# A two-block transformer kernel: the convolution in four segments, its order by hand, modulation loads placed anew, and a key normalisation queued behind the first scores

## The chip, the cores and the metric

The kernel runs on one core of one Trainium2 chip, all of it in fp32 accuracy. The metric is the device time of one execution in microseconds (us); before the change it is 986.46, the median of three runs (984.71 to 987.13). A measurement here is told apart from no change at about 0.3%.

## The reference

256 tokens of 1,024 channels go through a first block (stick-breaking attention, pooling and a gated unit, merged, then a feed-forward part) and through a second one of two layers. In layer 0 of the second block a conformer convolution mixes the tokens, in layer 1 an attention with 16 heads of 64 channels; each is followed by an MLP. Six modulation vectors per layer scale, shift and gate. Cut to what the change touches:

```
cond = silu(c)
mod = cond @ ada_w[i] + ada_b[i]                  # per layer: sh1, sc1, g1, sh2, sc2, g2
h = rms_norm(x, mix_norm_g[i]) * (1 + sc1) + sh1
# layer 0
a, g = split(h @ w_in + b_in, 2)
u = a * sigmoid(g)
u = causal depthwise convolution of u over the tokens, 31 taps, + dw_b
u = silu(layer_norm(u, ln_g, ln_b))
y = u @ w_out + b_out
# layer 1
q, k, v = split(h @ w_qkv, 3);  q, k = rms_norm per head
y = softmax(q k^T / 8 - slope * distance, causal) v @ w_o
x = x + g1 * y
h = rms_norm(x, mlp_norm_g[i]) * (1 + sc2) + sh2
x = x + g2 * (square(relu(h @ w1)) @ w2)
```

## The kernel before, in words

**Weights.** The 256 tokens are two tiles `t` of 128. All weights are streamed once, in halves of 1 MB: SP issues the load into one of three `raw` buffers (L335), ACT rounds it to `wH` (L364), DVE makes the rest `wL` (L365), and four pairs can be live. A product of accuracy fp32 is three fp32r matmuls per chunk of 128 rows: `wH` by the activations' high part (L464), `wL` by it (L465), `wH` by their low part (L466). `ts_job` (L531) is one such job, 128 tokens by 512 outputs over 1,024 inputs, 24 matmuls, with a bias row ahead of it in the convolution (`bias_rows`, L541).

**Modulation.** `ada_w` makes 48 more halves of the same stream. Each is multiplied by `cond` and summed on DVE, two accumulations of 128x1024 (L393). Where a group is complete, `ada_finish` brings it to a row by four matmuls with 32 output columns (L405) and sends it through DRAM; `ada_load` brings it back on 128 partitions. The table `PUSH` says how many such halves are queued behind which weight blocks.

**Convolution.** `hk` holds h. For two halves `n` of the channels and two token tiles there are a gate and a linear job (`cg`, `ca`); `glu` (L1071) multiplies them into `uu[n]`. The 31 taps are applied in a Fourier basis: `conv_fwd` transforms a segment of 128 tokens by plain fp32 matmuls (L1080), DVE multiplies the spectrum by the taps' cosine and sine tables (L1086, two products), and `conv_inv` transforms back (L1095), accumulating two matmuls per tile and segment onto the bias row. Three overlapping segments cover the tokens, so that a tile meets two of them: four pairs of tile and segment, eight forward and sixteen inverse matmuls, all 128x128 by 512 columns. `normed` (L1111) normalises a tile, `to_chan` transposes it (L1117), applies silu (L1121) and splits it for the output projection `co` (`two_by_two`, L903). In this stretch PE's order is written out by hand (`manual_schedule`); DVE's and ACT's are a scheduler's, by priority. `conv_load` (L919) brings the tables in during the feed-forward part of the first block and makes the taps' spectra by four matmuls of 31 rows (L931).

**Attention.** `qk_norm` (L1211) squares on ACT, sums on DVE, takes the power on POOL (L1217) and multiplies on DVE (L1219); `qk_trans` transposes. `at_scores` (L1234) makes a pair of heads' scores on PE (L1242), adds the distance on DVE (L1246), takes maxima (L1248, L1249), exponentials on ACT (L1250, L1251) and scales (L1253, L1254); `at_trans` transposes the result (L1263); `av` multiplies by v with 64 output columns a head (L1313, L1314).

## Time and profile before

| | us |
|---|---|
| median of three runs (lowest, highest) | 986.46 (984.71, 987.13) |
| profiled execution, its own time | 986.63 |
| its span | 984.9 |
| PE busy | 961.7, 98% of the span |
| DVE busy | 709.1, 72% |
| ACT busy | 545.3, 55% |

The rows further below come from the profiled execution. In a timeline a row is: start in us, duration in us, engine, line, operation, output<-inputs, tile (rows*columns and moving operand for PE), type, number of records run together, and in brackets the idle time before it and what ended it. A plain fp32 matmul makes two records, an fp32r one makes one. Matmuls overlap in the pipeline, so that the distance between two starts tells what one costs, not its duration. The granted clock (PEclk) is a share of TensorE's full 2.4 GHz; 0.5 is 1.2 GHz.

### The profile page before, as it was taken

What the parts mean: (1) busy time and instruction counts of PE and PEld (TensorE: products, weight loads), DVE (VectorE), ACT (ScalarE), POOL (GpSimd) and SP (SyncE); (2) the same over time, 40 slices, a digit from 0 to 9 for tenths busy, and PEclk for the clock granted to TensorE, in tenths of its full rate; (3) what the DMA queues carried; (4) which work ended last, traced back from release to release, by engine and by line L of the source; (5) the groups of instructions that cost most, each with busy time, mean ns of one, the idle gap of its engine ahead of it and who ended that gap; (6) DMA issues with size and microseconds to landing.
All of it is one profiled execution on the core that took longest, in us unless ns stands there. A gap on an engine that the chain in (4) does not pass through costs nothing.

```text
span 984.9 us, 12815 instructions
## 1 busy us (share of the span) xinstructions
PE 961.7 (98%) x4969; PEld 790.5 (80%) x4969; DVE 709.1 (72%) x914; ACT 545.3 (55%) x835; POOL 61.0 (6%) x88
## 2 busy tenths in 40 slices
PE   7999999999999999998999999999999999999998
PEld 5998889878788887874878888887876778888886
DVE  6768878787587777887677677768578576665553
ACT  5656764556555565523545655555576456555561
POOL 5002110010000000100000000001320000000000
PEclk9999999999899999999999999999999999999999
DMA  7887786579478986685258888875525356676531
GB/s 251 275 287 260 260 282 227 171 257 331 147 273 304 312 300 203 235 308 195 86 171 302 286 282 290 297 267 185 195 83 164 108 171 214 224 251 253 192 128 43
DMA packets 89732, 223.37 MB, mean 227 GB/s; under 512 B 4305, under 2 KB 8299, under 8 KB 89671
## 3 DMA queue, kind: packets, MB, share of 16 engines
q1 hardware_dynamic: 89670, 222.55, 65.6%
q8 instruction: 39, 0.64, 0.3%
q14 instruction: 23, 0.18, 0.1%
HBM read 221.44 MB, written 1.10 MB: 226 GB/s over the span
## 4 chain that ended last, share of the span: by engine, by line
PE 82%; DVE 10%; issue 2%; POOL 2%; ACT 2%; DMA 1%; POOLq 0%; SPq 0%; ACTq 0%
PE A L466 14%; PE A L464 14%; PE A L465 14%; PE B L479 14%; PE B L480 7%; PE A L479 5%; DVE wL L365 4%; PE A L480 2%; PE A L471 2%; PE A L472 2%; PE A L473 2%; POOL rst L549 1%; PE A L1095 1%; PE B L524 1%; DVE rs L568 1%
## 5 line engine op out<-in xcount | busy, mean ns | idle before, releaser
L365 DVE TENSOR_TENSOR wL<-raw,wH 128x1024 fp32r<-128x1024 f32 x306 | 362.0, 1219 | 122.0 <-ACT wH L364 120.8
L364 ACT ACTIVATE wH<-raw 128x1024 fp32r<-128x1024 f32 x306 | 307.3, 1051 | 186.9 <-PE A L466 119.3
L479 PE MATMUL B<-hHL,wH 128*128 128x512 f32 x576 | 204.1, 398 | 0.0
L480 PE MATMUL B<-hHL,wL 128*128 128x256 f32 x576 | 161.8, 281 | 0.0
L464 PE MATMUL A<-wH,hidH 128*128 128x512 f32 x384 | 152.3, 397 | 0.0
L466 PE MATMUL A<-wH,hidL 128*128 128x512 f32 x384 | 150.8, 393 | 0.0
L465 PE MATMUL A<-wL,hidH 128*128 128x512 f32 x384 | 150.6, 392 | 0.0
L464 PE MATMUL A<-wH,hHL 128*128 128x512 f32 (+1 forms) x336 | 130.9, 390 | 1.5 <-ACT wH L364 0.8
L479 PEld LDWEIGHTS B<-hHL,wH 128*128 128x128 f32 x576 | 108.3, 188 | 27.5 <-ACT wH L364 0.8
L465 PE MATMUL A<-wL,hHL 128*128 128x512 f32 (+1 forms) x336 | 129.0, 384 | 0.5 <-DVE wL L365 0.5
L466 PE MATMUL A<-wH,hHL 128*128 128x512 f32 (+1 forms) x336 | 129.5, 386 | 0.0
L393 DVE SCALAR_TENSOR_TENSOR acc<-raw,cond,acc 128x1024 f32<-128x1024 f32 x84 | 107.7, 1282 | 10.7 <-DMA raw<-in_ada_w_dram 9.8
L480 PEld LDWEIGHTS B<-hHL,wL 128*128 128x128 f32 x576 | 108.8, 189 | 0.7
L464 PEld LDWEIGHTS A<-wH,hidH 128*128 128x128 f32 x384 | 72.8, 190 | 18.9 <-issue 3.8
L466 PEld LDWEIGHTS A<-wH,hidL 128*128 128x128 f32 x384 | 72.6, 189 | 15.9
L465 PEld LDWEIGHTS A<-wL,hidH 128*128 128x128 f32 x384 | 72.9, 190 | 14.6
L464 PEld LDWEIGHTS A<-wH,hHL 128*128 128x128 f32 x336 | 63.6, 189 | 14.9 <-ACT wH L364 1.2
L465 PEld LDWEIGHTS A<-wL,hHL 128*128 128x128 f32 x336 | 63.8, 190 | 12.8 <-DVE wL L365 1.0
L466 PEld LDWEIGHTS A<-wH,hHL 128*128 128x128 f32 x336 | 63.8, 190 | 12.5 <-DVE hHL L519 0.4
L479 PE MATMUL A<-hHL,wH 128*128 128x512 f32 x192 | 68.1, 399 | 0.0
L986 ACT ACTIVATE rs<-B 128x256 f32<-128x256 f32 x72 | 27.1, 377 | 49.9 <-PE B L480 49.8
L480 PE MATMUL A<-hHL,wL 128*128 128x256 f32 x192 | 53.6, 279 | 0.0
(238 smaller groups left out, 1167.0 us busy)
## 6 DMA issues: line engine op xcount, KB each, us to landing
raw<-in_mlp_w_dram SPq DMA_DIRECT2D x64, 1024.0 KB
raw<-in_ada_w_dram SPq DMA_DIRECT2D x48, 1024.0 KB
raw<-in_w_in_dram SPq DMA_DIRECT2D x19, 1024.0 KB
raw<-in_w_ff_in_dram SPq DMA_DIRECT2D x16, 1024.0 KB
raw<-in_w_ff_out_dram SPq DMA_DIRECT2D x16, 1024.0 KB
raw<-in_attn_w_qkv_dram SPq DMA_DIRECT2D x12, 1024.0 KB
raw<-in_conv_w_in_dram SPq DMA_DIRECT2D x8, 1024.0 KB
ada<-mod SPq DMA_DIRECT2D x24, 256.0 KB
```

Of the source, the lines that this page charges most:

```text
L364: act(h[:, p:q, :], v[:, p:q, :], AF.Copy)
L365: nc.vector.tensor_sub(l[:, p:q, :], v[:, p:q, :], h[:, p:q, :].bitcast(F32))
L393: stt(acc, v[:, c, :], cond[:, k:k + 1], src, op0=ALU.mult, op1=ALU.add)
L464: mm(dst, lh(xc), wh, start=s0, stop=False)
L465: mm(dst, lh(xc), wl, start=False, stop=False)
L466: mm(dst, ll(xc), wh, start=False, stop=s1)
L471: mm(dst, wh, rh(xc), start=(i == 0), stop=False)
L472: mm(dst, wh, rl(xc), start=False, stop=False)
L473: mm(dst, wl, rh(xc), start=False, stop=(i == len(kcs) - 1))
L479: mm(dst, wh, km.HL[:, :, k, :], start=(k == 0), stop=False)
L480: mm(dst[:, 0:S], wl, km.HL[:, 0, k, :], start=False, stop=(k == KC - 1))
L986: act(r1[:, s, :], a[:, S:2 * S], AF.Copy)
```

## The change

The convolution takes four segments that each keep 64 tokens and do not share them: a segment's window is its 64 tokens and the ones before it. Segment 2 needs tokens of both tiles, so DVE copies the wanted halves of the products into a tile `mid` on the way. Each segment is one forward matmul per channel half; the inverse of a tile is four matmuls of 64 output columns, two segments by cosine and sine, onto the two halves of the rows. DVE and ACT follow the hand-written order too, two jobs are cut by an argument `mid=(cut, fn)`, and `pump(1)`, `limit=` place the weight steps. Modulation halves are queued elsewhere: two instead of six in the convolution, one more in the MLP's list, three behind the blocks of v; the load of layer 1's third segment moves behind the attention. The tables of the convolution lie and are loaded otherwise. In the attention one exponential of a single element stands ahead of the stage, and the last multiply of a normalisation is queued behind the first pair's maxima (`issue_after`). The diff, cut to its core; a line "..." stands for what is left out (the tables' contents, and removed code that the listing above shows):

```diff
@@ -30,20 +30,18 @@
-PUSH = {'pre': (0, 1, 0, 0, 0, 0), 'mix': (1, 2, 1, 2, 2, 1), 'ff': (1, 1, 1, 1, 1, 1, 1, 1, 1, 0, 1, 1, 1, 1, 1, 1), 'conv': (1, 4, 1), 'mlp': (1, 1, 1, 0, 1, 1, 1, 1, 1, 1, 1, 0, 1, 1, 0, 1), 'at': (0, 0, 0, 0)}
+PUSH = {'pre': (0, 1, 0, 0, 0, 0), 'mix': (1, 2, 1, 2, 2, 1), 'ff': (1, 1, 1, 1, 1, 1, 1, 1, 1, 0, 1, 1, 1, 1, 1, 1), 'conv': (0, 2, 0), 'mlp': (1, 1, 1, 0, 1, 1, 1, 1, 1, 1, 1, 1, 1, 1, 0, 1), 'at': (0, 0, 0, 0)}
-KEEP = SEG - PAD
+KEEP = 64
+NSEG = S // KEEP
...
@@ -249,6 +245,7 @@
             ada_push(PUSH["at"][2 * n + i])
     for n in range(2):
         B["av", n] = block512(I["attn_w_qkv_2"], 3 * D, 2 * D + n * 512)
+    ada_push(3)
     for n in range(2):
         B["ao", n] = block512(I["attn_w_o_2"], D, n * 512)
     for j in range(9):
@@ -528,11 +525,16 @@
                 self.from_token_half(t, b, src[b])
-    def ts_job(km, t, blk, n0=0, n1=512, bias=None):
+    def ts_job(km, t, blk, n0=0, n1=512, bias=None, mid=None):
         dst = bankA()
         if bias is not None:
             bias_rows(dst, bias)
-        ts(dst[:, :n1 - n0], km.h(t), km.l(t), blk, K8, n0, n1, start=bias is None)
+        cut = mid[0] if mid else KC
+        ts(dst[:, :n1 - n0], km.h(t), km.l(t), blk, K8[:cut], n0, n1, start=bias is None, stop=not mid)
+        if mid:
+            mid[1]()
+            ts(dst[:, :n1 - n0], km.h(t), km.l(t), blk, K8[cut:], n0, n1, start=False)
         return dst
...
@@ -900,12 +903,13 @@
-    def two_by_two(km, b0, b1, after, bias=(None, None)):
-        res = {}
+    def two_by_two(km, b0, b1, after, bias=(None, None), res=None):
+        res = dict(res or {})
         need(b0, b1)
         for t in range(NT):
             for n, b in enumerate((b0, b1)):
-                res[t, n] = ts_job(km, t, b, bias=bias[n])
+                if (t, n) not in res:
+                    res[t, n] = ts_job(km, t, b, bias=bias[n])
                 if t == 1:
                     if n == 0:
                         after(0, [res[0, 0], res[0, 1]])
@@ -918,19 +922,21 @@
     def conv_load():
         tb = I["conv_tables"]
-        cv["tab"] = T([P, TS_], "q4", 4)
-        nc.sync.dma_start(cv["tab"], dram(tb, 0, [[TI, P], [1, TS_]]))
-        cv["inv"] = T([P, len(PAIRS), 2, P], "gb", 2)
-        nc.sync.dma_start(cv["inv"], dram(tb, TS_, [[TI, P], [2 * P, len(PAIRS)], [P, 2], [1, P]]))
         dw = T([P, D], "q4", 4)
         nc.sync.dma_start(dw[:TAPS, :], dram(I["conv_dw_2"], 0, [[D, TAPS], [1, D]]))
-        cv["w"] = [T([P, D], "q4", 4) for _ in range(2)]
-        for j in range(2):
-            for n in range(2):
+        aux = T([P, TI - TF], "rs", 4)
+        nc.sync.dma_start(aux, dram(tb, TF, [[TI, P], [1, TI - TF]]))
+        cv["w"] = [T([P, 2, 512], "q4", 4)]
+        tab = T([P, TF], "q4", 4)
+        nc.sync.dma_start(tab, dram(tb, 0, [[TI, P], [1, TF]]))
+        cv["fwd"] = tab[:, :NSEG * P].rearrange("p (b n) -> p b n", b=NSEG)
+        cv["inv"] = tab[:, NSEG * P:].rearrange("p (t j n) -> p t j n", t=NT, j=2)
+        cv["w"].append(T([P, 2, 512], "q4", 4))
+        for n in range(2):
+            for j in range(2):
                 pt = bankB()
-                mm(pt, cv["tab"][:TAPS, TF + j * P:TF + (j + 1) * P], dw[:TAPS, n * 512:(n + 1) * 512],
-                   start=True, stop=True)
-                act(cv["w"][j][:, n * 512:(n + 1) * 512], pt, AF.Copy)
+                mm(pt, aux[:TAPS, j * P:(j + 1) * P], dw[:TAPS, n * 512:(n + 1) * 512], start=True, stop=True)
+                act(cv["w"][n][:, j, :], pt, AF.Copy)
         raw = T([P, 512], "rs", 4)
         for h in range(2):
             r = h * NB
@@ -1062,114 +1068,122 @@
     uu = [T([P, NT, 512], "hidH", 2) for _ in range(2)]
+    mid = T([P, 2, 512], "ok", 2)
     outs = {}
     spec = {}
...
+    SPEC_AT = {(0, 0): ("hidL", 2), (0, 1): ("hidL", 2), (0, 2): ("ok", 2), (0, 3): ("gb", 2),
+               (1, 0): ("q4", 4), (1, 1): ("q4", 4), (1, 2): ("ok", 2), (1, 3): ("ok", 2)}
+    def gate_of(t, n, **kw):
+        sg = ts_job(hk, t, B["cg", n], bias=2 + n, **kw)
+        g = T([P, 512], "rs", 4)
+        act(g, sg, AF.Sigmoid)
+        return g
+    def glu(t, n, g):
+        a = ts_job(hk, t, B["ca", n], bias=n)
+        vtt(uu[n][:, t, :], a, g, op=ALU.mult)
+        r = slice(KEEP - KEEP * t, P - KEEP * t)
+        vtt(mid[r, n, :], a[r, :], g[r, :], op=ALU.mult)
+    def conv_fwd(n, b):
+        s = bankB()
+        mm(s, cv["fwd"][:, b, :], mid[:, n, :] if b == 2 else uu[n][:, b // 2, :], start=True, stop=True)
+        pr = spec[n, b] = T([P, 2, 512], *SPEC_AT[n, b])
         for j in range(2):
...
+            vtt(pr[:, j, :], s, cv["w"][n][:, j, :], op=ALU.mult)
     st6 = [T([P, 2, 6], "bn", 2) for _ in range(NT)]
     tn = {}
+    def conv_inv(t, n):
+        o = outs[t, n] = bankB() if t else bankA()
+        bias_rows(o, 4 + n)
+        for j in range(2):
+            for i in range(2):
+                cs = slice(i * KEEP, (i + 1) * KEEP)
+                mm(o[cs, :], cv["inv"][:, t, j, cs], spec[n, 2 * t + i][:, j, :], start=False, stop=(j == 1))
     def stats(t, n):
         nc.vector.bn_stats(st6[t][:, n, :], outs[t, n])
...
+    def rstd(t):
         mv = T([P, 2], "ss", 4)
         nc.vector.bn_aggr(mv, st6[t])
...
+        tn[t] = mv, rstd_of([mv[:, 1:2]])
+    def normed(t):
+        mv, rs = tn[t]
+        tn[t] = []
         for b in range(2):
...
+            h = T([P, 512], "rs", 4)
+            vts(h, outs[t, b], mv[:, 0:1], rs, op0=ALU.subtract, op1=ALU.mult)
+            tn[t].append(h)
+    def to_chan(t, b):
+        pt = bankB()
+        for i in range(4):
+            nc.tensor.transpose(pt[:, i * P:(i + 1) * P], tn[t][b][:, i * P:(i + 1) * P], ident)
+        sl = T([P, 4, P], "rs", 4)
+        for i in range(4):
+            c = 4 * b + i
+            act(sl[:, i, :], pt[:, i * P:(i + 1) * P], AF.Silu, scale=col("lng", c), bias=col("lnb", c))
+        sk.split(sl, 4 * b, 4 * b + 4, t * P, (t + 1) * P)
+    ada_load(0, 4)
+    sk = KM((("hidL", "hidL"), ("hidH", "gb")))
+    co = {}
+    need(B["cg", 0], B["ca", 0])
+    with tc.manual_schedule(engines={nc.tensor.engine, nc.vector.engine, nc.scalar.engine}):
         for t in range(NT):
...
+            g = gate_of(t, 0)
             if t == 1:
...
+                done(B["cg", 0], limit=2)
+            glu(t, 0, g)
+        done(B["ca", 0], limit=2)
+        g = gate_of(0, 1)
+        for b in range(NSEG):
+            conv_fwd(0, b)
+        glu(0, 1, g)
+        for t in range(NT):
+            conv_inv(t, 0)
+            stats(t, 0)
+        pump(1)
         conv_fwd(1, 0)
...
+        conv_fwd(1, 1)
+        pump(1)
+        def inv01():
+            conv_inv(0, 1)
+            stats(0, 1)
+            rstd(0)
+        g = gate_of(1, 1, mid=(6, inv01))
+        done(B["cg", 1], limit=1)
+        normed(0)
+        glu(1, 1, g)
+        done(B["ca", 1], limit=1)
+        to_chan(0, 0)
         conv_fwd(1, 2)
...
+        conv_fwd(1, 3)
+        to_chan(0, 1)
+        pump(1)
+        def inv11():
+            conv_inv(1, 1)
+            stats(1, 1)
+            rstd(1)
+        co[0, 0] = ts_job(sk, 0, B["co", 0], bias=6, mid=(4, inv11))
+        pump(1)
         normed(1)
...
+        def chan1():
+            to_chan(1, 0)
+            to_chan(1, 1)
+        co[0, 1] = ts_job(sk, 0, B["co", 1], bias=7, mid=(6, chan1))
+    pump()
@@ -1180,7 +1194,7 @@
     ada_load(0, 3)
-    two_by_two(sk, B["co", 0], B["co", 1], after_mix(0), bias=(6, 7))
+    two_by_two(sk, B["co", 0], B["co", 1], after_mix(0), bias=(6, 7), res=co)
@@ -1190,7 +1204,6 @@
     ff(nk[-1], (("m1", 0), ("m2", 0)), after_mlp0,
        {2: lambda: ada_load(0, 5), 6: lambda: ada_load(1, 1, 0)})
-    ada_load(1, 2)
@@ -1204,6 +1217,7 @@
+    act(ada_one[0:1, 0:1], ada_one[0:1, 0:1], AF.Exp, scale=0.0)
@@ -1215,10 +1229,14 @@
         nc.vector.reduce_sum(ssq, sq.rearrange("p (h d) -> p h d", d=64), axis=AX.X)
         nc.gpsimd.tensor_scalar(ssq, ssq, EPS, None, op0=ALU.add)
         nc.gpsimd.tensor_tensor(ssq, ssq, neg_half.to_broadcast([P, 8]), op=ALU.pow)
-        qq = T([P, 512], "rs", 4)
-        vtt(qq.rearrange("p (h d) -> p h d", d=64), a.rearrange("p (h d) -> p h d", d=64),
-            ssq.rearrange("p (h o) -> p h o", o=1).to_broadcast([P, 8, 64]), op=ALU.mult)
-        return qq
+        def scaled():
+            qq = T([P, 512], "rs", 4)
+            vtt(qq.rearrange("p (h d) -> p h d", d=64), a.rearrange("p (h d) -> p h d", d=64),
+                ssq.rearrange("p (h o) -> p h o", o=1).to_broadcast([P, 8, 64]), op=ALU.mult)
+            return qq
+        return scaled
@@ -1246,7 +1264,9 @@
             stt(s, dist, -slopes[h], z[:, :384], op0=ALU.mult, op1=ALU.add)
             m = T([P, 2], "ss", 4)
             nc.vector.reduce_max(m[:, 0:1], s[:, 0:P], axis=AX.X, negate=True)
-            nc.vector.reduce_max(m[:, 1:2], s[:, P:384], axis=AX.X, negate=True)
+            top = nc.vector.reduce_max(m[:, 1:2], s[:, P:384], axis=AX.X, negate=True)
+            if i == 1 and state["top"] is None:
+                state["top"] = top
             act(s[:, 0:P], s[:, 0:P], AF.Exp, bias=m[:, 0:1], accum_out=sums[:, 0, h:h + 1])
             act(s[:, P:384], s[:, P:384], AF.Exp, bias=m[:, 1:2], accum_out=sums[:, 1, h:h + 1])
             nc.vector.reciprocal(sums[:, :, h:h + 1], sums[:, :, h:h + 1])
@@ -1267,7 +1287,7 @@
-    state = {"s": 0, "t": 0, "o": 0}
+    state = {"s": 0, "t": 0, "o": 0, "top": None}
@@ -1294,10 +1314,15 @@
                 if t == 1:
                     done(b)
                 flush(HOLD)
-                pend.append((n, t, i, qn))
+                state["top"] = None
                 if n == 1 and t + i > 0:
                     for _ in range(2):
                         at_step(8)
+                if state["top"] is None:
+                    pend.append((n, t, i, qn()))
+                else:
+                    with tc.issue_after(state["top"].ins):
+                        pend.append((n, t, i, qn()))
@@ -1338,7 +1363,7 @@
     while state["o"] < 16:
         at_step(16)
         av_next(16)
-    ada_load(1, 4, 3)
+    ada_load(1, 2, 4, 3)
     two_by_two(ok, B["ao", 0], B["ao", 1], after_mix(1))
```

Where rows move, three places. First PE in the convolution, the first inverse matmuls and what stands around them (`uu` is hidH, the spectra are rs before, and hidL, ok and gb now; the bias row is brow). Before:

```order
L466 MATMUL A_3878<-wH_3736,hHL_3490 128x512
L1080 MATMUL B_3920<-hidH_3638,q_367_2446 128x512
L1095 MATMUL A_3874<-rs_3870,gb_2448 128x512
L1095 MATMUL A_3874<-rs_3872,gb_2448 128x512
L541 MATMUL A_3929<-brow_2481,pick_2473 128x512
L1095 MATMUL A_3929<-rs_3870,gb_2448 128x512
L1095 MATMUL A_3929<-rs_3872,gb_2448 128x512
L1080 MATMUL B_3933<-hidH_3639,q_367_2446 128x512
L541 MATMUL A_3939<-brow_2481,pick_2473 128x512
```

Now:

```order
L463 MATMUL A_3837<-wH_3781,hHL_3490 128x512
L543 MATMUL A_3865<-brow_2481,pick_2473 128x512
L1105 MATMUL A_3865<-hidL_3819,q_370_2451 64x512
L1105 MATMUL A_3865<-hidL_3824,q_370_2451 64x512
...
L543 MATMUL B_3872<-brow_2481,pick_2473 128x512
L1105 MATMUL B_3872<-ok_3829,q_370_2451 64x512
L1105 MATMUL B_3872<-gb_3834,q_370_2451 64x512
...
L1091 MATMUL B_3883<-hidH_3635,q_370_2451 128x512
L1091 MATMUL B_3888<-hidH_3635,q_370_2451 128x512
L543 MATMUL A_3897<-brow_2481,pick_2473 128x512
```

Before, a tile's inverse stands in pieces between jobs, each matmul 128 columns wide; now its four 64-column ones follow each other on one bias row, both tiles in a row, ahead of the forward matmuls of the other channel half.

Second DVE in the convolution, from the spectra of column half 1 to the normalisation of the first tile (wL is a weight step, acc a modulation accumulation, bn the statistics, A and B are PSUM banks). Before:

```order
L1086 TENSOR_TENSOR rs_3978<-B_3975,q_370_2452 128x512
L1086 TENSOR_TENSOR rs_3980<-B_3975,q_371_2453 128x512
L1086 TENSOR_TENSOR rs_3984<-B_3982,q_370_2452 128x512
L1086 TENSOR_TENSOR rs_3986<-B_3982,q_371_2453 128x512
L1103 BN_STATS bn_3643<-A_3971 128x6
L1107 BN_AGGR ss_3991<-bn_3643 128x2
L548 TENSOR_SCALAR rst_3993<-ss_3991 128x1
L1111 TENSOR_SCALAR hidL_3996<-A_3874,ss_3991,rst_3993 128x512
L1111 TENSOR_SCALAR hidL_3996<-A_3971,ss_3991,rst_3993 128x512
L1103 BN_STATS bn_3644<-A_3999 128x6
```

Now, the statistics and spectra, and further on the product for `mid` (ok) with its spectra:

```order
L1108 BN_STATS bn_3638<-A_3865 128x6
L1108 BN_STATS bn_3639<-B_3872 128x6
L390 SCALAR_TENSOR_TENSOR acc_3402<-raw_3743,cond_84,acc_3402 128x1024 x2
L1094 TENSOR_TENSOR q_599_3885<-B_3883,q_371_2453 128x512 x2
L1094 TENSOR_TENSOR q_601_3890<-B_3888,q_371_2453 128x512 x2
L390 SCALAR_TENSOR_TENSOR acc_3402<-raw_3779,cond_84,acc_3402 128x1024 x2
L1108 BN_STATS bn_3638<-A_3917 128x6
...
L1085 TENSOR_TENSOR hidH_3635<-A_3949,rs_3935 128x512
L1087 TENSOR_TENSOR ok_3637<-A_3949,rs_3935 64x512
L362 TENSOR_TENSOR wL_3978<-raw_3881,wH_3977 128x1024 x2
L516 TENSOR_TENSOR hidL_3996<-rs_3990,hidL_3995 128x4x128
L1094 TENSOR_TENSOR ok_4001<-B_3999,q_371_2453 128x512 x2
```

The accumulations now stand in front of the spectra of column half 1 and of the last statistics of tile 0, and two weight steps and a split stand between `mid` and its spectra.

Third DVE in the attention, at the first pair of heads (w are the scores, ss the maxima, ssq the norms). Before:

```order
L1215 TENSOR_REDUCE ssq_6058<-junk_6059 128x8
L1219 TENSOR_TENSOR rs_6064<-A_6033,ssq_6058 128x512
L1246 SCALAR_TENSOR_TENSOR w_965_6078<-cst_5806,B_6072 128x384
L1246 SCALAR_TENSOR_TENSOR w_967_6088<-cst_5806,B_6073 128x384
L1248 TENSOR_REDUCE ss_6080<-w_965_6078 128x1
L1249 TENSOR_REDUCE ss_6080<-w_965_6078 128x1
...
L1246 SCALAR_TENSOR_TENSOR w_971_6104<-cst_5806,B_6098 128x384
L1246 SCALAR_TENSOR_TENSOR w_973_6114<-cst_5806,B_6099 128x384
```

Now:

```order
L1229 TENSOR_REDUCE ssq_6046<-junk_6047 128x8
L1264 SCALAR_TENSOR_TENSOR w_959_6064<-cst_5793,B_6058 128x384
L1264 SCALAR_TENSOR_TENSOR w_961_6074<-cst_5793,B_6059 128x384
L1266 TENSOR_REDUCE ss_6066<-w_959_6064 128x1
L1267 TENSOR_REDUCE ss_6066<-w_959_6064 128x1
L1266 TENSOR_REDUCE ss_6076<-w_961_6074 128x1
L1267 TENSOR_REDUCE ss_6076<-w_961_6074 128x1
L1264 SCALAR_TENSOR_TENSOR w_965_6090<-cst_5793,B_6084 128x384
...
L1267 TENSOR_REDUCE ss_6102<-w_967_6100 128x1
L1235 TENSOR_TENSOR rs_6116<-A_6021,ssq_6046 128x512
```

The multiply (rs<-A,ssq) that stood ahead of the first pair's scores now stands behind the second pair's maxima.

## Rows read from the trace of the kernel before

**Rows 1.** The page, engines: busy time, share of the span, instructions.
```profile
PE 961.7 (98%) x4969; PEld 790.5 (80%) x4969; DVE 709.1 (72%) x914; ACT 545.3 (55%) x835; POOL 61.0 (6%) x88
```

**Rows 2.** PE's waits: who waits for whom; total us, times, longest.
```profile
PE B L524 <- DVE rs L575: 4.0, 5, 1.2
```

**Rows 3.** PE's timeline through the convolution.
```profile
393.33 0.40 PE L541 MATMUL A<-brow,pick 128*128 128x512 f32 x1
...
399.02 0.40 PE L541 MATMUL A<-brow,pick 128*128 128x512 f32 x1
...
450.44 1.88 PE L1095 MATMUL A<-rs,gb 128*128 128x512 f32 x4
452.24 0.50 PE L541 MATMUL A<-brow,pick 128*128 128x512 f32 x1
...
457.88 1.98 PE L1095 MATMUL A<-rs,gb 128*128 128x512 f32 x4 [0.85 <-DVE rs L1086]
...
466.43 0.50 PE L464 MATMUL A<-wH,q 128*128 128x512 f32 x1 [1.56 <-ACT q L518]
468.43 0.66 PE L1117 MATMUL B<-ident,hidL 128*128 128x128 f32 x4 [1.50 <-DVE hidL L1111]
...
492.36 0.39 PE L464 MATMUL A<-wH,hHL 128*128 128x512 f32 x1
```

**Rows 4.** PE's timeline at four matmuls of 32 output columns.
```profile
277.80 1.06 PE L405 MATMUL B<-acc,onesr 128*32 128x512 f32 x8
278.80 0.50 PE L464 MATMUL A<-wH,hidH 128*128 128x512 f32 x1
279.13 0.39 PE L465 MATMUL A<-wL,hidH 128*128 128x512 f32 x1
```

**Rows 5.** PE's timeline in the product with v, 64 output columns.
```profile
773.39 0.65 PE L1313 MATMUL A<-q,gb 128*64 128x256 f32 x4
773.82 0.44 PE L1314 MATMUL A<-q,gb 128*64 128x128 f32 x4
```

**Rows 6.** ACT's timeline at the convolution's first silu.
```profile
457.90 1.28 ACT L1121 ACT_TABLE_LOAD   x1 [4.77 <-DVE rs L1086]
464.00 1.85 ACT L1121 ACTIVATE rs<-B,cols 128x128 f32<-128x128 f32 x5 [4.82 <-PE B L1117]
```

**Rows 7.** Line L393: durations min/median/max in ns; its waits in us, times.
```profile
L393 DVE SCALAR_TENSOR_TENSOR acc<-raw,cond,acc x84: 1265/1277/1422, 52.7 to 896.1; 128x1024 f32<-128x1024 f32 x84
...
  DMA raw<-in_ada_w_dram: 11.0, 7
```

**Rows 8.** Timelines of DVE, ACT and PE at the attention's first pair.
```profile
716.96 0.69 DVE L1219 TENSOR_TENSOR rs<-A,ssq 128x512 f32<-128x512 f32 x1 [2.11 <-POOL ssq L1217]
717.57 1.01 DVE L1246 SCALAR_TENSOR_TENSOR w<-cst,B 128x384 f32<-128x384 f32 x2
...
718.85 1.28 ACT L1250 ACT_TABLE_LOAD   x1 [4.14 <-DVE ss L1248]
...
716.23 0.50 PE L465 MATMUL A<-wL,hHL 128*128 128x512 f32 x1
...
719.80 0.39 PE L465 MATMUL A<-wL,hHL 128*128 128x512 f32 x1
721.99 0.61 PE L1263 MATMUL B<-ident,w 128*128 128x128 f32 x3 [1.80 <-DVE w L1253]
```

**Rows 9.** Stretches: length, busy us (instructions) of PE, PEld, DVE, ACT, POOL; PEclk, DMA share, GB/s.
```profile
252.00:258.00 6.00, 6.00 (x13) 4.13 (x13) 4.29 (x5) 2.93 (x5) 0.00 (x0) 0.50 0.80 281
722.00:726.00 4.00, 4.00 (x14) 3.17 (x15) 3.08 (x11) 3.52 (x12) 0.00 (x0) 0.58 0.00 0
768.00:776.00 8.00, 8.00 (x62) 6.30 (x61) 5.22 (x5) 6.63 (x10) 0.00 (x0) 1.00 0.36 110
```

**Rows 10.** PE's timeline at the taps' four matmuls.
```profile
248.57 4.26 PE L931 MATMUL B<-q,q 31*128 31x512 f32 x8
```

More of the change, by code (lines that the diff above doesn't have):

```diff
@@ L710, in net_kernel @@
         rs = rstd_of([ssg[:, t:t + 1]])
-        stt(gvt[:, t, :], gvt[:, t, :], rs, gmg, op0=ALU.mult, op1=ALU.mult)
-    done(B["gv"])
+        last = stt(gvt[:, t, :], gvt[:, t, :], rs, gmg, op0=ALU.mult, op1=ALU.mult)
+    with tc.issue_after(last.ins):
+        done(B["gv"])
     need(B["u"])
@@ L1089, in conv_inv @@
-    def conv_inv(t, n, b):
-        i = PAIRS.index((t, b))
-        if (t, n) not in outs:
-            outs[t, n] = bankA()
-            bias_rows(outs[t, n], 4 + n)
-        for j in range(2):
-            mm(outs[t, n], cv["inv"][:, i, j, :], spec[n, b, j], start=False, stop=(j == 1 and b == t + 1))
-    ada_load(0, 4)
-    sk = KM((("q4", "q4"), ("q4", "q4")))
+    SPEC_AT = {(0, 0): ("hidL", 2), (0, 1): ("hidL", 2), (0, 2): ("ok", 2), (0, 3): ("gb", 2),
+               (1, 0): ("q4", 4), (1, 1): ("q4", 4), (1, 2): ("ok", 2), (1, 3): ("ok", 2)}
```

117 lines of the change are left out of this document (19 added, 98 removed).

## The prediction

> **What bounds it now.** I read the page first: PE is busy 961.7 us of the span of 984.9, DVE 709.1 [rows 1]. So the end is set by the amount of PE work plus the places where PE stands, and DVE and ACT matter only where PE waits for them. The view of PE's waits came next: the named waits are few and short, the costliest group 4.0 us over five [rows 2], in places that the change leaves alone. Those it touches are single: three in the convolution [rows 3] and one in the attention [rows 8], each under 2 us. Then PE's timeline through the convolution, from the first bias row (393.33) to the first matmul of the following MLP (492.36): 99.0 us [rows 3].
>
> What this stretch holds, by rows: twelve jobs of a bias row and 24 matmuls, 5.69 us each from bias row to bias row (393.33 to 399.02), 68.3 in all. Four inverse matmuls from 450.44 to the bias row at 452.24 take 1.80, less 0.08 of settling: 0.43 for each of two passes, 0.86 for a plain fp32 matmul with 512 moving columns. Sixteen of these are 13.8 us, the eight forward ones 6.9. Of the rest, 0.85 + 1.56 + 1.50 = 3.9 us are idle before the rows at 457.88, 466.43 and 468.43 [rows 3].
>
> **The change, part by part, against the profiled execution of 986.63 us** (0.17 above the median of the three runs, 986.46).
>
> *Narrow inverse matmuls.* Still sixteen of 512 moving columns, but each now fills 64 of the 128 output columns, and neighbours in the queue write opposite halves. What they cost hangs on whether two halves run at once. The convolution before shows no such pair; two other places do. The modulation rows are four matmuls of 32 output columns, two passes each; alone they would need 4 x 0.86 = 3.44, and the next line starts 1.00 after them (277.80 to 278.80) [rows 4]. In the attention's product with v, four records of 64 columns by 256, two matmuls of 0.43 each, take 0.43 together (773.39 to 773.82) [rows 5]. So I take eight pairs at 0.86 = 6.9 in place of 13.8. The bounds are no overlap (gain 0) and 6.9. Going to narrow columns and back has a price: the four took 0.14 more than 0.86, and the first full matmul behind them 0.33 to the next start instead of 0.23 [rows 4], so 0.24 for each of four groups, 1.0. **Gain 5.9.** The Trainium skill says in "TensorEngine Tiling (Array Packing)", Key Properties, that changing the tiling mode drains TensorE, which speaks against mixing four narrow groups into full-width work. It gives no duration; if the drain were a matmul's whole streaming time at each of eight switches, 8 x 0.43 = 3.4, the gain would be 3.5. The rows above hold both switches of a group in 0.24, and I go by them.
>
> *The hand-written order of PE, DVE and ACT.* The three waits, 3.9 us, were PE standing behind spectrum products, behind the first silu chain (table load of 1.28, five steps from 464.00) and behind the second normalisation [rows 3, 6]. Now the first transposes stand behind lin(1,1), and two matmul jobs are cut so that the inverse and the second half's transposes lie in their middle. Those waits go. What is late next is the forward matmul of segment 2 in column half 1: it reads `mid`, which DVE makes last, after the product for `uu`, both of at most 0.7 (half of an accumulation's 1.28 for half the elements [rows 7]), both behind lin(1,1)'s end; after four transposes (about 0.4) PE has nothing else. I put that at 1.3 to 2.1. The silu chain before the first job of the output projection leaves 0.4 to 0.6 more, since the table load (1.28) and four silus with their copy run beside two forward matmuls and four transposes only. Together 2.1, bounds 0.5 and 3.9 (as much as today). **Gain 3.9 - 2.1 = 1.8.** The convolution then ends at about 492.36 - 7.7 = 484.7 on the old scale.
>
> *What is added on DVE and hidden:* four products for `mid`, and the accumulations on the new schedule, 1.28 each [rows 7]. DVE is 72% busy [rows 1]. Fewer modulation loads now stand between blocks of the convolution (two in place of six), so its DMA and DVE load falls; this I cost at nothing, since PE's matmuls cover it, and if that cover is gone it is the second rival.
>
> *Attention, first pair of heads.* DVE's multiply of the key normalisation (716.96) stood ahead of the first pair's scores and had waited 2.11 for POOL; the scores' pass started at 717.57, ACT then loaded its exp table for 1.28 (718.85), and PE stood until 721.99, 1.80 idle [rows 8]. With the multiply behind the pair's maxima, the scores' pass can start when PE has finished the scores, before the next job's matmul at 716.23, so 1.3 earlier; the table is loaded in the MLP before. The transposes could then go at 721.99 - 1.3 - 1.28 = 719.4. PE comes to them at 719.80 + 0.23 = 720.03. The 1.80 vanishes. Behind it PE's granted clock was 0.58 of full over 722 to 726 [rows 9], which is the 1.2 GHz level for most of it, and costs 4 x 0.42 = 1.7. PE had been idle right before; with the idle gone I expect full clock. **Gain 3.5**, bounds 1.3 (part of a wait left, clock still falls) and 3.8. The moved multiply is wanted only for key transposes behind six more matmuls of the next job, so nobody queues behind it in earnest.
>
> *Modulation loads into the attention.* Three halves, six accumulations of 1.28 = 7.7 us on DVE [rows 7], beside a run of 41 matmuls between two score pairs, 41 x 0.227 = 9.3 us by the job's rate [rows 3]. They fit, but DVE is also to make probabilities there. Cost 0.5, bounds 0 and 3 (a third of them exposed, with a short stand). Where they come from, the end of the first MLP, DVE was under PE's matmuls: no gain there. Their modulation rows move with them, 1.0 [rows 4] in either place.
>
> *Filter tables.* The table with the taps' cosines now comes through the small pool that the hidden layer uses, and its DMA is issued behind three weight halves; its four matmuls, at 248.57 in this trace [rows 10], stand 61 matmuls later in PE's order, so about 14 us, which is about when it can land. Cost 0.5, bounds 0 and 3. After these four narrow matmuls, 31 rows by 128, the clock is 0.50 over 252 to 258 [rows 9]. They are still four in a row, so I leave these 3.0 in place.
>
> **Sum:** 986.6 - 5.9 - 1.8 - 3.5 + 0.5 + 0.5 = 976.4; as the profiled execution is 0.2 above the median, **976.2 us**.
>
> **Rivals.**
> 1. *The halves don't pair* as fp32 accumulation alternates between them. For: no row shows 64 columns by 512. Against: both narrow cases in the trace do overlap [rows 4, 5]. Time: 976.2 + 5.9 = 982.1. Chance 0.08.
> 2. *In-order DVE gives the convolution back.* By hand, a pair of accumulations stands in front of the spectrum products, and the next pair in front of the statistics; each waits for a load. In the trace DVE stood 11.0 us in seven waits for that DMA, 1.6 each [rows 7]. Two of them, PE behind each, are 3.2, and a clock that falls after each stand as at 722 costs 1.7 more: 6.6 in all, 982.8. It takes loads that land later than PE's 5.7 us jobs allow. Against: the stretch has fewer loads now. Chance 0.14.
> 3. *Slower: the clock falls after every narrow group.* Four 31-row matmuls were followed by six microseconds at 0.50, 3.0 us lost, and 0.4 more at the edges by my estimate [rows 9, 10]. If each of the four groups of half-width matmuls does that: 4 x 3.4 = 13.6, so 989.8. From three groups on (10.2) the gain is gone. Against: at 64 columns the product with v holds 1.00 over 768 to 776 [rows 9], though it fills both halves. Chance 0.05.
> 4. *The taps' stretch keeps full clock* in its new place, between other matmuls: 3.4 less, 972.8. Chance 0.11.
>
> **How the numbers follow.** The forecast case has 0.62. Its own bounds (conv 1 either way, attention -0.3 to +2.2, tail and tables up to 3 each, seldom together) reach from 974 to 980. The fourth rival opens the range to 971 below, the first two to 983 above: **970.5 to 983**, which leaves out the third and the worst of the second. A measurement of this kernel tells about 0.3%, 3 us, from no change, so faster is below 983.5 and slower above 989.4. Faster: 0.62 + 0.11 + nearly all of 0.08 + two thirds of 0.14 = 0.89. Slower: the third rival and a little of the rest, 0.05. Within: 0.06.
>
> **What would show it.** Right: two records of neighbouring halves of the inverse start together, and four matmuls with their bias row take about 2.2 instead of 3.7; the three convolution waits are gone and one of 1 to 2 us stands before a forward matmul; the first matmul of the MLP comes 7 to 8 us earlier after the first bias row (91 instead of 99); no table load in the attention, no 1.8 before its first transposes, a clock of 1.0 behind them. Wrong: a convolution stretch above 95 us, inverse matmuls 0.86 apart, DVE waits for modulation loads with PE behind them, or a granted clock below 1 inside the convolution.

## The result

| | us |
|---|---|
| changed kernel, median of four runs (lowest, highest) | 973.75 (973.28, 976.32) |
| kernel before on the same chip, median (lowest, highest) | 986.65 (984.71, 987.13) |
| ratio, with its 95% interval | 0.9879 (0.9862 to 0.9896) |
| profiled execution of the changed kernel, its own time | 976.32 |
| its span | 974.6 |

The kernel is 1.2% faster, with 976.2 forecast. The profiled execution happens to be the longest of the four; the sum of the prediction for that execution was 976.4. Why the other runs are shorter is told with the filter tables further below.

The page, engines of the changed kernel, which answers to [rows 1]:

```profile
PE 956.8 (98%) x4969; PEld 785.8 (81%) x4969; DVE 713.7 (73%) x922; ACT 546.5 (56%) x836; POOL 59.2 (6%) x88
```

PE's timeline through the convolution after the change, which answers to [rows 3]: first bias row, a group of four inverse matmuls between two bias rows, the wait for `mid`, the first job of the output projection, the first matmul of the MLP.

```profile
394.91 0.40 PE L543 MATMUL A<-brow,pick 128*128 128x512 f32 x1
...
434.13 0.39 PE L543 MATMUL A<-brow,pick 128*128 128x512 f32 x1
434.45 1.94 PE L1105 MATMUL A<-hidL,q 128*64 128x512 f32 x8
436.32 0.50 PE L543 MATMUL B<-brow,pick 128*128 128x512 f32 x1
436.75 0.64 PE L1105 MATMUL B<-ok,q 128*64 128x512 f32 x1
436.76 0.64 PE L1105 MATMUL B<-gb,q 128*64 128x512 f32 x1
...
455.69 1.13 PE L1091 MATMUL B<-ok,q 128*128 128x512 f32 x2 [0.94 <-DVE ok L1087]
...
458.08 0.47 PE L543 MATMUL A<-brow,pick 128*128 128x512 f32 x1
458.39 0.44 PE L461 MATMUL A<-wH,hidL 128*128 128x512 f32 x1
...
486.34 0.40 PE L461 MATMUL A<-wH,hHL 128*128 128x512 f32 x1
```

The stretch is 486.34 - 394.91 = 91.43 us, against 99.03 [rows 3]. Matmuls onto the two halves start 0.01 apart (436.75, 436.76), and a group of four takes 1.87 (434.45 to 436.32). Of the three waits of before none is left; the new one of 0.94 is for segment 2.

PE's timeline at the attention's first transposes after the change, which answers to the last of [rows 8], and the stretch behind them with its clock, which answers to the second of [rows 9]:

```profile
711.18 0.40 PE L462 MATMUL A<-wL,hHL 128*128 128x512 f32 x1
711.81 0.61 PE L1283 MATMUL B<-ident,w 128*128 128x128 f32 x3 [0.23 <-DVE w L1273]
```

```profile
712.00:716.00 4.00, 4.00 (x23) 3.33 (x22) 3.96 (x12) 3.70 (x12) 0.00 (x0) 1.00 0.02 4
```

The wait is 0.23 in place of 1.80, and the clock is full behind it in place of 0.58.

PE's waits for the normalised rows of the MLPs and the attention, which answer to [rows 2]:

```profile
PE B L521 <- DVE rs L577: 2.8, 4, 1.2
```

The prediction took this group as left alone; it falls from 4.0 to 2.8. Two waits behind the convolution make the difference, 0.87 before 499.51 and 0.56 before 684.90 in the kernel before, none and 0.26 now.

So the span's 984.9 - 974.6 = 10.3 us divide so: the convolution begins 394.91 - 393.33 = 1.6 later, takes 7.6 less, and what lies behind its end takes (984.9 - 492.36) - (974.6 - 486.34) = 4.3 less. Of the 4.3, the first transposes' wait is 1.6 and the clock behind it 1.7; the two waits just named are as large as the rest. The 1.6 ahead of the convolution can't be put down to the change: both profiles have a stretch at half clock behind the taps, and eleven further profiles of the changed kernel and its variants, none of which has it, begin the convolution between 389.56 and 391.18, as far apart as this.

### The profile page after: what moved, and what is told of

Same layout as the page of the kernel before. It is cut to its first block, busy times and chain, and to the rows that moved or that the text cites. A ratio compares the mean times of both kernels' runs of the same rounds, so it can differ in the third digit from the quotient of the medians.

```text
span 974.6 us, 12820 instructions
## 1 busy us (share of the span) xinstructions
PE 956.8 (98%) x4969; PEld 785.8 (81%) x4969; DVE 713.7 (73%) x922; ACT 546.5 (56%) x836; POOL 59.2 (6%) x88
## 4 chain that ended last, share of the span: by engine, by line
PE 82%; DVE 10%; issue 2%; DMA 2%; POOL 2%; ACT 2%; POOLq 0%; SPq 0%; ACTq 0%
PE B L476 14%; PE A L463 14%; PE A L462 14%; PE A L461 14%; PE B L477 7%; PE A L476 5%; DVE wL L362 4%; PE A L477 2%; PE A L468 2%; PE A L469 2%; PE A L470 2%; POOL rst L551 1%; PE B L521 1%; PE B L1091 1%; DVE rs L570 1%
## 5 line engine op out<-in xcount | busy, mean ns | idle before, releaser
L476 PE MATMUL B<-hHL,wH 128*128 128x512 f32 x576 | 206.8, 402 | 0.0
L461 PE MATMUL A<-wH,hidH 128*128 128x512 f32 x400 | 157.0, 394 | 0.0
L463 PE MATMUL A<-wH,hidL 128*128 128x512 f32 x400 | 156.3, 391 | 0.0
L462 PE MATMUL A<-wL,hidH 128*128 128x512 f32 x400 | 156.2, 390 | 0.1
L461 PEld LDWEIGHTS A<-wH,hidH 128*128 128x128 f32 x400 | 75.0, 188 | 18.1 <-issue 1.7
L463 PEld LDWEIGHTS A<-wH,hidL 128*128 128x128 f32 x400 | 75.1, 188 | 16.8 <-DVE hidL L516 0.7
L462 PEld LDWEIGHTS A<-wL,hidH 128*128 128x128 f32 x400 | 75.2, 188 | 16.2 <-issue 0.8
```

The lines of the kernel that those rows point to most:

```text
L461: mm(dst, lh(xc), wh, start=s0, stop=False)
L462: mm(dst, lh(xc), wl, start=False, stop=False)
L463: mm(dst, ll(xc), wh, start=False, stop=s1)
L476: mm(dst, wh, km.HL[:, :, k, :], start=(k == 0), stop=False)
```

## The experiments

The experiments ran on three chips in three groups of four, each in turn with the kernel before, whose 30 runs in this part lie between 984.14 and 988.78 us (medians 986.57, 986.80 and 987.22). A ratio is to the kernel before on the same chip. Two further measures come from the profiles: the stretch from the convolution's first bias row to the MLP's first matmul, and the time from there to PE's last matmul. The latter lies between 482.90 and 484.44 us in the seven profiles whose code behind the stretch is that of the changed kernel; a difference of 1.5 us there is not told apart from none.

**The changed kernel again.** No edit.

> The changed kernel once more, as the measure for the next three on the same chip. Expected: 973 to 976 us, 91.4 us from the first bias row of the convolution to the first matmul of the MLP, four narrow inverse matmuls in 1.9 us. The time differs by up to 3.4 us with a stretch at half clock behind the taps' four matmuls, which one profiled run had and another seems not to have had; if that is so, a run whose granted clock is 1.00 behind the taps is the shorter one by that much.

Measured: median 971.92, ratio 0.9859 (0.9839 to 0.9879). The convolution takes 481.68 - 390.19 = 91.49. PE's timeline, first bias row and first matmul of the MLP:

```profile
390.19 0.40 PE L543 MATMUL A<-brow,pick 128*128 128x512 f32 x1
...
481.68 0.40 PE L461 MATMUL A<-wH,hHL 128*128 128x512 f32 x1
```

The same six microseconds, behind the taps, by stretches; first the earlier profile of the changed kernel:

```profile
268.00:274.00 6.00, 6.00 (x19) 4.86 (x19) 1.89 (x3) 1.29 (x3) 0.00 (x0) 0.50 0.86 323
```

then this one:

```profile
268.00:274.00 6.00, 6.00 (x36) 5.26 (x36) 2.31 (x5) 1.69 (x4) 0.00 (x0) 1.00 0.64 222
```

Same code, 19 matmuls against 36 in six microseconds: the clock's fall behind the taps is there in one run and not in the other. Of the eight runs of the changed kernel, two have a mean granted clock of 0.996 (975.03 and 976.32 us), the others 0.998 to 1.0 and 970.94 to 974.2 us. Only the run of 976.32 was profiled of those two; that the other's loss is the same one is read from its mean clock.

**The inverse at full width.**

```diff
-        t, cols = b // 2, slice((b % 2) * KEEP, (b % 2 + 1) * KEEP)
-        inv[:64, t, 0, cols], inv[64:, t, 0, cols] = c, d
-        inv[:64, t, 1, cols], inv[64:, t, 1, cols] = d, -c
+        i, cols = b % 2, slice((b % 2) * KEEP, (b % 2 + 1) * KEEP)
+        inv[:64, i, 0, cols], inv[64:, i, 0, cols] = c, d
+        inv[:64, i, 1, cols], inv[64:, i, 1, cols] = d, -c
...
-                mm(o[cs, :], cv["inv"][:, t, j, cs], spec[n, 2 * t + i][:, j, :], start=False, stop=(j == 1))
+                mm(o, cv["inv"][:, i, j, :], spec[n, 2 * t + i][:, j, :], start=False, stop=(j == 1 and i == 1))
```

> Sixteen inverse matmuls of 128 output columns, each with zeros in the half that is not its segment's; all else as changed. Theory (two halves run at once): a group of four takes 3.4 to 3.5 instead of 1.86, the convolution stretch 97.5 to 98 instead of 91.4, the time 6 us more than the changed kernel. Rival (the new order is what pays, the inverse was hidden beside DVE's spectra anyway): stretch and time within 1.5 us of the changed kernel.

Measured: median 979.26, ratio 0.9929 (0.9913 to 0.9945). PE's timeline at the second group, and the ends of the stretch:

```profile
432.07 0.80 PE L543 MATMUL B<-brow,pick 128*128 128x512 f32 x1
432.70 1.02 PE L1104 MATMUL B<-ok,q 128*128 128x512 f32 x2
433.56 1.02 PE L1104 MATMUL B<-gb,q 128*128 128x512 f32 x2
434.42 1.02 PE L1104 MATMUL B<-ok,q 128*128 128x512 f32 x2
435.28 1.02 PE L1104 MATMUL B<-gb,q 128*128 128x512 f32 x2
436.13 1.88 PE L1091 MATMUL B<-hidH,q 128*128 128x512 f32 x4
...
486.86 0.40 PE L461 MATMUL A<-wH,hHL 128*128 128x512 f32 x1
```

The four start 0.86 apart and take 3.43 (432.70 to 436.13). From the first bias row (389.56) the stretch is 97.30, that is 5.81 more than in the run beside it. The prediction's first rival is out: the halves do pair, and that is worth 5.8, not the 6.9 of eight matmuls; I read the remaining 1.1 as what narrow groups among full-width matmuls cost, 0.27 a group. The medians differ by more, 7.3; behind the stretch the two profiles differ by 1.2 (484.44 against 483.24), no more than such profiles do.

**The four matmuls ordered by half.**

```diff
-        for j in range(2):
-            for i in range(2):
+        for i in range(2):
+            for j in range(2):
```

> The four narrow matmuls of a group ordered by half: cosine and sine of the first segment, then cosine and sine of the second, so that neighbours in the queue write the same half. If only neighbours can pair in the order of the queue: the second and third overlap, a group takes about 2.6 instead of 1.86, 3 us more in all. If PE looks further ahead or each half has a queue of its own: 1.9, no difference. If nothing pairs then: 3.4 to 3.5, 6 us more.

Measured: median 971.39, ratio 0.9859 (0.9837 to 0.9882); stretch 91.48. PE's timeline at the second group:

```profile
432.21 0.64 PE L1105 MATMUL B<-ok,q 128*64 128x512 f32 x1
432.23 0.64 PE L1105 MATMUL B<-gb,q 128*64 128x512 f32 x1
432.69 0.59 PE L1105 MATMUL B<-ok,q 128*64 128x512 f32 x1
432.71 0.59 PE L1105 MATMUL B<-gb,q 128*64 128x512 f32 x1
```

In the program two matmuls of the first segment (ok) now precede both of the second (gb); on the engine they run side by side all the same. The halves need not be neighbours in the queue.

**Hand-written order for PE alone.**

```diff
-    with tc.manual_schedule(engines={nc.tensor.engine, nc.vector.engine, nc.scalar.engine}):
+    with tc.manual_schedule(engines={nc.tensor.engine}):
```

> In the convolution only PE keeps the hand-written order; DVE's and ACT's are left to the scheduler by priority. Theory (the order by hand of the two others is worth something): waits of PE for spectra, for mid or for the silu chain come back, stretch 93 to 96 instead of 91.4. Rival (PE's own new order does it, the others would find the same): stretch within 1 us of 91.4. The other sign is possible too: the wait for mid (0.94 in the changed kernel) gets shorter where the scheduler puts the product ahead of a weight step.

Measured: median 974.26, ratio 0.9891 (0.9866 to 0.9916). PE's timeline, the same two places:

```profile
452.16 1.13 PE L1091 MATMUL B<-ok,q 128*128 128x512 f32 x2 [1.58 <-DVE ok L1087]
...
455.57 0.50 PE L461 MATMUL A<-wH,hidL 128*128 128x512 f32 x1 [0.57 <-ACT hidL L515]
...
483.48 0.40 PE L461 MATMUL A<-wH,hHL 128*128 128x512 f32 x1
```

From the first bias row (390.72) the stretch is 92.76, 1.3 more, by waits of 1.58 and 0.57 where the changed kernel has 0.94 and next to none. The order of DVE and ACT by hand is worth 1.3 of the 7.6, less than was expected. Behind the stretch one of the two normalisation waits of the kernel before is back as well (0.80 before 490.80); the medians differ by 2.3. No run showed the prediction's second rival, DVE giving the convolution back.

**No early table load.**

```diff
-    act(ada_one[0:1, 0:1], ada_one[0:1, 0:1], AF.Exp, scale=0.0)
```

> The changed kernel without the single-element exponential ahead of the attention; the deferred multiply stays. In the changed kernel the first scaled probabilities come 0.2 late (PE's wait 0.23 us). Theory (table load and deferral add up on the path): ACT loads its table for 1.28 between the first maxima and the first exponential, PE stands 1.4 to 1.6 us before the first transposes, and the clock falls to about 0.6 for the 4 us behind it, which costs 1.7 more; 3 us in all, 975. Rival (the clock's fall has another cause): 1.3 us more and a clock of 1.0.

Measured: median 974.64, ratio 0.9876 (0.9857 to 0.9896); the two of its four runs with a clock of 0.999 and 1.0 took 972.71 and 972.92. ACT's timeline, then PE's:

```profile
705.56 1.28 ACT L1269 ACT_TABLE_LOAD   x1 [2.25 <-DVE ss L1265]
706.85 0.40 ACT L1269 ACTIVATE w<-w,ss 128x128 f32<-128x128 f32 x1
```

```profile
708.70 0.30 PE L1282 MATMUL B<-ident,w 128*128 128x128 f32 x1 [0.41 <-DVE w L1272]
```

The load is back, but PE's wait is 0.41 and not 1.4: in this run's order 14 matmuls of the next job stand ahead of the transposes, in place of 10. That the scheduler does so because it reckons with the load is likely and not shown. The clock behind holds 1.00. Both theories missed the size, and no cost of the load alone is told apart from none: the time behind the stretch is 484.05, and 484.04 in a run that has the early load (the taps on 128 rows, in the changed kernel).

**The multiply ahead of the scores again.**

```diff
-                state["top"] = None
+                pend.append((n, t, i, qn()))
...
-                if state["top"] is None:
-                    pend.append((n, t, i, qn()))
-                else:
-                    with tc.issue_after(state["top"].ins):
-                        pend.append((n, t, i, qn()))
```

> The changed kernel with the key normalisation's multiply ahead of the first scores again; the table is loaded early. The multiply waits about 2.1 for POOL in front of the first pair's scores. Theory: scores 1.3 later, PE stands 1.5 us before the first transposes, clock falls behind it, 1.3 to 3.2 us more than the changed kernel (972 in the last runs). Rival (only the table load mattered): wait under 0.5, time the same.

Measured: median 978.79, ratio 0.9925 (0.9901 to 0.9949), lowest 977.21. DVE's timeline, PE's, and two stretches:

```profile
706.19 0.69 DVE L1235 TENSOR_TENSOR rs<-A,ssq 128x512 f32<-128x512 f32 x1 [2.11 <-POOL ssq L1231]
706.80 1.01 DVE L1264 SCALAR_TENSOR_TENSOR w<-cst,B 128x384 f32<-128x384 f32 x2
```

```profile
710.18 0.30 PE L1281 MATMUL B<-ident,w 128*128 128x128 f32 x1 [2.47 <-DVE w L1271]
...
724.67 0.55 PE L1281 MATMUL B<-ident,w 128*128 128x128 f32 x3 [1.98 <-ACT q L1247]
```

```profile
710.00:714.00 4.00, 3.81 (x22) 3.25 (x22) 4.00 (x16) 3.57 (x11) 0.00 (x0) 1.00 0.02 4
...
724.00:728.00 4.00, 3.33 (x12) 2.79 (x13) 2.35 (x5) 3.48 (x6) 1.90 (x2) 0.75 1.02 338
```

The wait comes back larger than it was before the change, and a second of 1.98 follows. The time behind the stretch is 488.73 against 483.24, 5.5 more and not 1.3 to 3.2: 2.2 of the first wait, 1.6 of the second (0.41 in the changed kernel) and 1.7 of the clock. Behind the stand of 2.47 the clock stayed at 1.00, behind that of 1.98 it fell: a stand of 2 us is followed by a fall in one place and not in another.

**The three modulation halves out of the attention.**

```diff
-    ada_push(3)
...
-'conv': (0, 2, 0), 'mlp': (1, 1, 1, 0, 1, 1, 1, 1, 1, 1, 1, 1, 1, 1, 0, 1)
+'conv': (0, 2, 1), 'mlp': (1, 1, 1, 1, 1, 1, 1, 1, 1, 1, 1, 1, 1, 1, 1, 1)
...
+    ada_load(1, 2)
     hk = nk[-1]
...
-    ada_load(1, 2, 4, 3)
+    ada_load(1, 4, 3)
```

> The three modulation halves taken out of the attention again and queued in the first MLP and behind the output projection's blocks, and their row loaded before the attention; all else as changed. Theory (the move costs and brings nothing: DVE has room in both places): within 1 us of the changed kernel. Rival (six accumulations in the attention's queue hold up scores): 1 to 3 us less. Other rival (the move took DVE work out from in front of the MLP's normalisation): 1 us more.

Measured: median 973.47, ratio 0.9872 (0.9853 to 0.9891); stretch 91.94 (389.88 to 481.82). Beside the changed kernel's 971.92, on another chip, that is some 1.5 more, which the intervals do not separate; it does not say that the move costs or gains anything. One wait does answer to it. PE's timeline ahead of the attention:

```profile
675.19 0.63 PE L520 MATMUL B<-ident,rs 128*128 128x128 f32 x4 [0.56 <-DVE rs L576]
```

That is the 0.56 of the kernel before, where the changed kernel has 0.26. It is of the kind that the other rival names, and 0.3 of its 1 us.

**The taps on 128 rows, in the kernel before.**

```diff
+        nc.gpsimd.memset(dw, 0.0)
...
-                mm(pt, cv["tab"][:TAPS, TF + j * P:TF + (j + 1) * P], dw[:TAPS, n * 512:(n + 1) * 512],
+                mm(pt, cv["tab"][:, TF + j * P:TF + (j + 1) * P], dw[:, n * 512:(n + 1) * 512],
```

> The kernel before with one edit: the taps' four matmuls take 128 rows (the 97 added ones are zeros) in place of 31, same columns, same time at full clock. All runs of the kernel before so far show a mean granted clock of 0.994 to 0.997, the changed kernel 0.998 to 1.0 in most and 0.996 in few; the stretch at 0.50 behind the taps is 3.4 us, 0.0035 of the mean. Theory (few rows in use let the clock fall): no stretch at 0.50 behind the taps, mean clock up by 0.003, 983.3. Rival (plain fp32 as such or the place lets it fall): clock 0.995 and 986.6 as before.

Measured: median 984.17, ratio 0.9975 (0.9964 to 0.9987). PE's timeline at the taps, and the stretch behind:

```profile
247.83 3.60 PE L932 MATMUL B<-q,q 128*128 128x512 f32 x8
250.86 0.79 PE L464 MATMUL A<-wH,hidH 128*128 128x512 f32 x1
```

```profile
250.00:256.00 6.00, 6.00 (x25) 4.44 (x24) 5.64 (x6) 4.18 (x8) 0.00 (x0) 1.00 0.68 210
```

The fall to 0.50 over 252 to 258 [rows 9] is gone from this profile, with the same place, the same columns and the same number of matmuls; what differs is the rows, and one operation on POOL that writes the zeros. The median is 2.6 lower and the interval excludes 1, so the edit pays, and the few rows are the likely reason for the fall. It is not quite shown: the profiled run is the shortest of the seven, and two others (984.88 and 984.84) have mean clocks of 0.995 and 0.996, as the kernel before has; where those lost it was not profiled.

**Both attention edits undone.** The two edits above together.

> The changed kernel with both attention edits undone (table loaded at its first use, multiply ahead of the first scores); convolution and loads as changed. Theory (the two together are the 3.5 us of the forecast): PE stands 1.8 us before the first transposes and the clock is about 0.58 for the 4 us behind, 975 to 976 against 971.5 for the changed kernel without a stretch at half clock behind the taps. Rival (with the new loads the attention has slack elsewhere): under 973. Other rival: more, as the run with the deferral alone undone took 977.5 and had two waits of 2.5 and 2.0.

Measured: median 977.98, ratio 0.9914 (0.9893 to 0.9935). PE's waits, and the stretch with its clock at the first of them, which ends at 710.89:

```profile
PE B L1280 <- DVE w L1270: 2.4, 1, 2.4
...
PE B L402 <- DVE acc L390: 1.1, 1, 1.1
```

```profile
710.00:714.00 4.00, 3.11 (x13) 2.49 (x14) 3.10 (x14) 4.00 (x16) 0.00 (x0) 0.78 0.00 0
```

The wait of 2.4 and a clock below 1 behind it are the expected ones, and a wait that the changed kernel does not have stands beside them: PE for the modulation accumulations that were moved here. The two edits are worth 6 in the changed kernel (489.53 behind the stretch against 483.24), more than the forecast's 3.5. The waits of 2.4 (0.23 with the edits) and 1.1 and the clock's 1.7 make 5.0 of it; the rest I have not traced. The run is no slower than the one with the multiply alone undone (978.79), which again leaves nothing that is told apart for the table load. That the accumulations are late because they were moved is argued: no run undid the edits with the three halves elsewhere.

**The taps on 128 rows, in the changed kernel.** The edit as above, on `aux`.

> The changed kernel with the taps' four matmuls on 128 rows. In the changed kernel and its variants the stretch at half clock behind the 31-row matmuls was there in about one run of four, judged by a mean clock of 0.996 or less. Theory (few rows let the clock fall, and in the new place only by chance): all runs at 0.998 to 1.0, 971.5, none at 975. Rival (the chance is in something else): one run of four still at 0.996 and 975 to 976.

Measured: median 971.58, lowest 970.41, highest 972.35 (five runs), ratio 0.9838 (0.9823 to 0.9853); all five clocks at 0.999 or 1.0. None is above 975. The intervals of this and of the changed kernel overlap, so no gain at the median is shown. Nine runs have the taps on 128 rows (these and the four of the combined run below), all at 0.999 or 1.0; of the 34 runs with 31 rows that keep the deferred multiply, nine are at 0.997 or less. At that rate nine clean runs would come by chance about one time in sixteen: a hint for the theory, not a proof.

**`mid` before `uu`**, a single run.

```diff
-        vtt(uu[n][:, t, :], a, g, op=ALU.mult)
         r = slice(KEEP - KEEP * t, P - KEEP * t)
         vtt(mid[r, n, :], a[r, :], g[r, :], op=ALU.mult)
+        vtt(uu[n][:, t, :], a, g, op=ALU.mult)
```

> The changed kernel with the product for mid ahead of the one for uu on DVE. Theory (PE's 0.94 before segment 2's forward matmul is the wait for the second of two products of 0.7): the wait falls to 0.3, the stretch from 91.45 to 90.9. Rival (uu is then late for segment 3): the wait moves to the next forward matmul by as much, stretch the same.

Measured: 972.47, stretch 91.45. PE's timeline:

```profile
451.36 1.12 PE L1091 MATMUL B<-ok,q 128*128 128x512 f32 x2 [0.34 <-DVE ok L1086]
452.32 1.02 PE L1091 MATMUL B<-hidH,q 128*128 128x512 f32 x2
453.94 0.66 PE L1126 MATMUL B<-ident,rs 128*128 128x128 f32 x4 [0.61 <-ACT rs L1130]
```

The wait for `mid` falls by 0.60, and 0.61 turns up two steps on, where PE waits for ACT's silu. Neither theory had that: not `uu` is late next, but the silu chain.

**Combined:** taps on 128 rows, `mid` first, and the second transposes ahead of the forward matmuls.

```diff
         to_chan(0, 0)
+        pt01 = trans(0, 1)
         conv_fwd(1, 2)
         conv_fwd(1, 3)
-        to_chan(0, 1)
+        to_chan(0, 1, pt01)
```

> The changed kernel with three edits: taps on 128 rows, mid before uu, and the transposes of the second normalised half ahead of the forward matmuls of segments 2 and 3. Expected: wait before segment 2's forward matmul under 0.1, stretch 90.4 to 90.7 instead of 91.45, no stretch at half clock in any run: 970 to 970.8, against 971.5 to 976 of the changed kernel. If the transposes only move the wait behind them (DVE's spectra come no earlier): 971.5.

Measured: median 971.57 (970.99 to 971.98), ratio 0.9840 (0.9826 to 0.9854), stretch 91.54. ACT's timeline and PE's:

```profile
449.84 1.28 ACT L1136 ACT_TABLE_LOAD   x1 [1.76 <-issue]
451.14 1.51 ACT L1136 ACTIVATE rs<-B,cols 128x128 f32<-128x128 f32 x4
```

```profile
452.70 1.13 PE L1092 MATMUL B<-hidH,q 128*128 128x512 f32 x2 [1.46 <-ACT rs L1136]
```

The wait for `mid` is gone, and PE waits 1.46 for ACT one step on: nothing that this forward matmul reads comes from ACT, so I take it that it waits for a bank of B that the first silus, done at 452.65, still read. ACT has stood 1.76 us ahead of its silu table load, which comes with the first silu. What ends last at this place is that load and the four silus behind it; to load the table ahead of time, as the attention now does, was not tried here. The expected 970 to 970.8 was missed.

## Why the prediction was right

The measured 973.75 lies inside the range, just below the 974 to 980 of the forecast case and on the side of the fourth rival. That the profiled execution meets the sum (976.32 against 976.4) is partly luck: the convolution gave what was put (7.6, forecast 7.7), but what lies behind it gave 1.3 more than was put (4.3, forecast 3.5 less 0.5), and its start came 1.6 later where 0.5 was put.

**The halves pair (gain 5.9).** 5.8 by the run at full width, which is 6.9 less 1.1 for four narrow groups where 1.0 was put. The rows of 32 and of 64 columns elsewhere in the kernel [rows 4, 5] were good for it. The 3.5 that a streaming time for each switch would have left is out, since both switches of a group cost at most 0.27 (1.1 over four groups). The Trainium skill states a drain on a change of tiling mode ("TensorEngine Tiling (Array Packing)", Key Properties), without a price; here it is at most these 0.27 a group.

**The hand-written order (gain 1.8).** 7.6 - 5.8 = 1.8, as forecast, of which the run with PE's order alone gives 1.3 to DVE's and ACT's. The waits left were put too high: 0.94 for `mid` in place of 1.3 to 2.1, and next to none for silu in place of 0.4 to 0.6. By the two profiles, PE's idle time in the stretch fell by 2.8, from 4.4 to 1.6 (0.53 of either is a wait in the second job that the prediction did not count). Against it, summed from the distances of the starts without the waits, the 288 weight matmuls take 67.4 us in place of 66.4, for a reason that no run shows. So the 1.8 is partly luck: 2.8 of waits gained where 1.8 was put, less 1.0 of slower matmuls where nothing was put.

**Attention (gain 3.5, tail -0.5).** All that lies behind the convolution's end gained 4.3. The wait went from 1.80 to 0.23, the clock behind it from 0.58 to 1.00, as forecast, which together is 3.3. The step that failed in part is the reason given for the clock, that it falls behind a stand of PE: at the same place it stayed up behind 2.47 us in one run and fell behind 2.4 in another. The deferral carries the gain; the early table load by itself has none that is told apart.

**Modulation loads into the attention.** Put at a cost of 0.5, with 7.7 us of DVE beside 9.3 of matmuls. They fit with the attention edits in place; with those undone, PE waits 1.1 for the accumulations. "No gain" where they come from was not quite right: a wait of 0.56 ahead of the attention fell to 0.26, and is back in the run with the halves in the MLP.

**Filter tables (cost 0.5, low clock left in place).** This is the step that was wrong, and the main reason that the median is 2.4 below the forecast. The fourth rival (0.11) had the case in most runs: in the new place the clock falls behind the taps in few runs only, two of eight by their mean clocks. The profiled execution was one of those two; the others of its four are 2.1 to 3.0 shorter, where the rival put 3.4. That the four matmuls still stood in a row was no ground for leaving the loss in place, and why the new place pays it seldom is open: nine of the ten profiles with 31 rows in the new place have no fall behind the taps. The old place pays it in the profile, and all 30 runs of it in the experiments have a mean clock of 0.994 to 0.997. The 0.5 for the later tables is not shown: the taps start at 264.11, 15.5 later, without a wait.

**The rivals.** The first and second are out by the runs above. The third, a fall of the clock behind each narrow group, is out as well: after the change the convolution stretch holds 1.00.

```profile
394.90:486.30 91.40, 89.79 (x385) 64.61 (x384) 69.93 (x93) 40.32 (x64) 5.31 (x5) 1.00 0.47 157
```

## What to carry to other kernels

Matmuls that need only half of the output columns can be had two at a time, here at a price of at most 0.27 us a group among full-width work; a place elsewhere in the same trace where narrow matmuls overlap tells this before it is built. An operation that waits on an in-order engine costs what stands behind it, so look at what a normalisation that is wanted late stands in front of. When one wait is taken away, ask which chain is ready next: here two edits at one place moved PE's wait from DVE (0.94) to ACT (1.46) and left the stretch as it was.
